# A hybrid mixer block on one core: a fifth pair of gate products by seven multiplications, sums moved into accumulating DMAs, and other steps at both ends

## The chip, the core and the metric

The kernel runs on one core of a Trainium2 chip. The core has a matrix engine (TensorE, PE in the profile; its weight loads are PEld), VectorE (DVE), ScalarE (ACT), GpSimd (POOL) and SyncE (SP). Each takes its own instructions in program order and waits on semaphores for the others. SP, ACT and POOL can issue DMAs, which run on 16 DMA engines. The metric is device microseconds of one execution; the time before is the median of three runs.

## What is computed

One decoder block for 256 tokens of width 2048, all in float32, cut to what matters here:

```python
def hybrid_mixer(h, w_in, ...):
    proj = jnp.einsum('bsd,de->bse', h, w_in)
    (q, k, v, g_out, gk_low, gate_b, gate_c, xc, merge_a, merge_b) = jnp.split(proj, SPLIT_IDX, axis=-1)
    ...
    y_a = (o * jax.nn.silu(g_out...))                                  # o: gated linear attention, normalised
    y_b = gate_b * causal_depthwise_conv(gate_c * xc, conv_w)          # y_t = sum_j w[j] u_{t-2+j}, j = 0..2
    merged = jax.nn.sigmoid(merge_a) * y_a + jax.nn.sigmoid(merge_b) * y_b
    return jnp.einsum('bse,ed->bsd', merged, w_out)

def swiglu(h, w_gate_up, w_down):
    gate, up = jnp.split(jnp.einsum('bsd,df->bsf', h, w_gate_up), [FFN_HIDDEN], axis=-1)
    return jnp.einsum('bsf,fd->bsd', jax.nn.silu(gate) * up, w_down)

h = x + hybrid_mixer(rmsnorm(x, mix_norm_w), ...)
h = h + swiglu(rmsnorm(h, ffn_norm_w), ...)
return rmsnorm(h, final_norm_w)
```

## The kernel before

**Weights as pieces.** All weights are read once or a little more, in pieces of 128 x 1024 floats (512 KB). A piece holds two row blocks of 128 for 512 columns (`n = 2`), or four for 256. Each piece is split for the matrix engine into a rounded high part `hi` (ScalarE, `high`, line 238) and a low part `lo = raw - hi` (VectorE, `low`, line 243), and each product is three matmuls, `mm3`, lines 347 to 349. `load_piece` runs up to five pieces ahead (`LOOK = 5`); there are five raw buffers, six for `hi`, five for `lo`.

**Entries and ticks.** `stream_list` lays down the order of all pieces. One piece used is one entry, and `used()` counts a tick after it. `later(d, f)` runs f's instructions d ticks on, `at(t, f)` at tick t, `one_at_a_time(d, f)` queues transposes that come d ticks on at the earliest and two ticks apart. These calls fix where an instruction stands in the program order of its engine. `pin` holds it there.

**Eights and sevens.** A group of 512 columns with 16 row blocks is done in one of two ways. As *eights* it has 8 entries of 12 matmuls (2 row blocks, 2 token blocks, 3 matmuls). As *sevens* two groups are done together by seven block products in place of eight: 28 entries of 6 matmuls. `seven_list` gives them in order: for each of four quarters q, 11, t1, t3, t2, t4, and then eight entries 21 and 22. The four t entries of a quarter are sums of weight blocks, formed on VectorE (lines 259 and 265) ahead of the split; the blocks for 21 and 22 are loaded a second time. So a pair of sevens has 24 loads and 16 sums, against 16 loads as eights. Its five accumulators `pa` to `pe` stand in PSUM banks b0 to b4, starting at bank 2n mod 5 for the n-th pair (`sevens`, line 402). Two are read at the end of the quarters, token block 1 being done after t4 of quarter 3 (`done(1, ...)`, line 429), token block 0 after the last entry (lines 435 and 436). `mixed` puts eights between the sevens: after each t entry, then after 21 and 22. Eights, down products and transposes use three other banks (`lent`); plain groups such as `wo0` take banks from a running count (`bank`, modulo 6, from wo0 on modulo 5).

**The gate stage.** For each of four blocks i of 512 columns there are six groups: gc and xc (their product is `us[i]`, the input of the convolution), gb, g, ma, mb. Four pairs (gc, xc) are sevens; everything else is eights. `gates_list` orders them by `GATES`: g0 alone, then each pair with 24, 24, 24 and 32 eights, and gb3 and mb3 alone at the end, 240 entries. When a pair is done, `conv(i)` copies `us[i]` one and two tokens down with six DMAs on POOL (lines 843 to 848) into `u1` and `u2`, and from 12 ticks on (`CONV_AT`) VectorE does three products with the taps and two adds (line 856). `merge(i)` multiplies by `sb[i]` (gb times the sigmoid of mb), adds `ya[i]` one tick later and queues two transposes of the result, which give `mh[i]`, `ml[i]` for the product with w_out. `wo0` follows as plain eights.

**The second half.** The other three wo groups, eight pairs of sevens (fg, fu) and the down products follow (`hidden_list`). A down product's two accumulators are added to the residual `h` by VectorE (line 1043). The last part of the down products runs alone (`down_list`), token block 0 ahead of 1 in its last group; `finish(t)` computes the last norm of a token block, scales and stores it in three parts.

**The start.** `hooks` puts the loads of x transposed (`start`) between the halves of the first weight piece (k0), and the small table `cols` behind the first of them on SP.

Of the kernel before, what the change touches and what calls it, by code (L numbers as in the profile page):

```python
# [8 lines left out]
F32 = mybir.dt.float32  # L9
# [3 lines left out]
ALU = mybir.AluOpType  # L13
# [30 lines left out]
def plan():  # L44
# [28 lines left out]
GATES = (  # L73
    (None, ("g0",)),
    (("gc0", "xc0"), ("ma0", "gb0", "mb0")),
    (("gc1", "xc1"), ("g1", "ma1", "gb1")),
    (("gc2", "xc2"), ("mb1", "g2", "ma2")),
    (("gc3", "xc3"), ("gb2", "mb2", "g3", "ma3")),
    (None, ("gb3", "mb3")),
)  # L80
# [26 lines left out]
def mixed(pair, eights, early=False):  # L107

    if pair is None:
        return eights  # L110
# [4 lines left out]
    while rest > 0:  # L115
        for some in (sums + ("11",) if early else sums, ("21", "22")):
# [68 lines left out]
def block_kernel(ctx, tc, x, xt, cols_in, gkw_in, gku_in, gnw, conv_w, finw, w_in, w_out, w_gu, w_dn, out):  # L185
# [82 lines left out]
    def load_piece():  # L268
# [4 lines left out]
        if i < len(stream):  # L273
            key, k0 = stream[i]
            if isinstance(k0, tuple):
                n, w = 2, 512
                raw = sum_of(key, *k0)
                step = n
            else:
# [3 lines left out]
                step = n // 2 if i == 0 else n  # L283
# [4 lines left out]
            else:  # L288
                if i == 0:
                    piece[1] = wlo.tile([P, n, w], F32R, tag="lo", name="lo")  # L290
                for a in range(0, n, step):
                    b = a + step
# [219 lines left out]
    def start(xs, a, b):  # L512
        nc.sync.dma_start(xs[:, 0:b - a, :], xt[:, a * T:b * T].rearrange("p (k t) -> p k t", t=T))
        if a == 0:
            nc.sync.dma_start(cols, cols_in)
# [17 lines left out]
    hooks[(0, 0)] = lambda: start(xs0, 0, 2)  # L533
# [299 lines left out]
    us, ya, sb, merge_at = {}, {}, {}, {}  # L833

    def conv(i):
        u = us[i]
# [4 lines left out]
        nc.gpsimd.memset(u1[0:1, 0, :], 0.0)  # L841
        nc.gpsimd.memset(u2[0:2, 0, :], 0.0)
        nc.gpsimd.dma_start(u1[1:113, :, :], u[0:112, :, :])
        nc.gpsimd.dma_start(u2[2:114, :, :], u[0:112, :, :])
        nc.gpsimd.dma_start(u1[113:128, :, :], u[112:127, :, :])
        nc.gpsimd.dma_start(u2[114:128, :, :], u[112:126, :, :])
        nc.gpsimd.dma_start(u1[0:1, 1, :], u[127:128, 0, :])
        nc.gpsimd.dma_start(u2[0:2, 1, :], u[126:128, 0, :])

        def taps_of(j):  # L850
            return taps[:, j:j + 1, :].to_broadcast([P, NT, 512])
# [326 lines left out]
```

## Time and profile before

| | us |
|---|---|
| median of 3 runs | 1507.53 (1506.82 to 1507.73) |
| the profiled execution, its own time | 1505.39 |
| its span, first to last instruction | 1503.7 |
| TensorE busy | 1488.9 |
| VectorE busy | 1277.6 |
| ScalarE busy | 862.9 |
| DMA traffic | 358.58 MB, 238 GB/s in the mean |

A busy time is the union of an engine's instructions. Matmuls overlap, so their lengths add up to more than TensorE's busy time. A row of the groups ("line engine op out<-in xcount | busy, mean ns | idle before, releaser") gives the sum and mean of one kind of instruction and what ended the idle time before it. A row of the windows gives the busy time of each engine in a stretch from the span's start. "us to landing" is from a DMA's issue to its last byte.

### The profile page before, as it was taken

Reading aid. Unit: us, or ns where it says so; the run is one execution under the profiler, and the core shown is the slowest. Engines: PE = TensorE matmul, PEld = TensorE weight load, DVE = VectorE, ACT = ScalarE, POOL = GpSimd, SP = SyncE. Lnnn points to the kernel's source line nnn. Section 1 sums busy time; section 2 is a strip of 40 time slices with the busy share of each in tenths; the row PEclk is TensorE's granted clock in tenths of the full one; section 3 lists DMA queues with packets and bytes.
Section 4 is the critical chain, followed back from the end, with each engine's and each line's share of the span. In section 5 each row is a group of like instructions: output and inputs, shape, how many; then the busy total and the mean of one; then the engine's idle time right before and its main releaser. Section 6 shows DMA issues by size and latency. Waiting matters only on the chain.

```text
span 1503.7 us, 19350 instructions
## 1 busy us (share of the span) xinstructions
PE 1488.9 (99%) x7057; PEld 1244.0 (83%) x7057; DVE 1277.6 (85%) x1280; ACT 862.9 (57%) x975; POOL 33.1 (2%) x60
## 2 busy tenths in 40 slices
PE   9999999999999999999999999999999999999997
PEld 8989988888887888888888888888888788888886
DVE  5885869979979879966689999999999999999975
ACT  6864546655655655654566756655565556565553
POOL 0010000000000000000000000000000000000000
PEclk9999999999999999999999999999999999999999
DMA  9755557877877877786676777777877777786782
GB/s 312 239 171 171 178 162 257 283 229 234 283 261 232 296 247 248 252 261 214 211 222 214 238 249 252 252 263 226 268 238 238 256 265 273 243 268 224 241 288 84
DMA packets 99984, 358.58 MB, mean 238 GB/s; under 512 B 11476, under 2 KB 11604, under 8 KB 99760
## 3 DMA queue, kind: packets, MB, share of 16 engines
q1 hardware_dynamic: 96656, 346.88, 70.0%
q0 software_dynamic: 2800, 8.89, 2.2%
q10 hardware_dynamic: 432, 1.57, 0.3%
q8 instruction: 55, 0.90, 0.2%
q14 instruction: 41, 0.34, 0.1%
HBM read 351.03 MB, written 2.10 MB: 235 GB/s over the span
## 4 chain that ended last, share of the span: by engine, by line
PE 95%; DVE 2%; issue 1%; ACT 1%; DMA 0%; SPq 0%; DVEq 0%; ACTq 0%
PE fg L347 8%; PE fg L349 8%; PE fg L348 8%; PE dn L347 5%; PE dn L349 5%; PE dn L348 5%; PE gc L347 3%; PE gc L348 3%; PE gc L349 3%; PE wo L347 2%; PE wo L349 2%; PE v L347 2%; PE gb L347 2%; PE wo L348 2%; PE v L348 2%; PE v L349 2%
## 5 line engine op out<-in xcount | busy, mean ns | idle before, releaser
L243 DVE TENSOR_TENSOR lo<-raw,hi 128x1024 fp32r<-128x1024 f32 (+1 forms) x505 | 611.6, 1219 | 114.3 <-ACT hi L238 32.3
L238 ACT CAST hi<-raw 128x1024 fp32r<-128x1024 f32 (+1 forms) x505 | 523.9, 1048 | 272.5 <-PE gb L349 25.9
L238 ACT CAST hi<-x 128x1024 fp32r<-128x1024 f32 x144 | 151.7, 1053 | 263.5 <-DVE x L265 201.0
L243 DVE TENSOR_TENSOR lo<-x,hi 128x1024 fp32r<-128x1024 f32 x144 | 176.1, 1223 | 37.8 <-ACT hi L238 26.3
L347 PE MATMUL dn<-lo,acth 128*128 128x512 f32 (+1 forms) x368 | 140.7, 382 | 1.7 <-DVE h L1043 0.9
L349 PE MATMUL dn<-hi,acth 128*128 128x512 f32 (+1 forms) x368 | 139.9, 380 | 0.0
L348 PE MATMUL dn<-hi,actl 128*128 128x512 f32 (+1 forms) x368 | 139.8, 380 | 0.0
L265 DVE TENSOR_TENSOR x<-x,raw 128x1024 f32<-128x1024 f32 x96 | 117.0, 1219 | 11.3 <-DMA raw<-in_w_in_dram 6.2
L347 PE MATMUL fg<-lo,hh 128*128 128x512 f32 x288 | 112.4, 390 | 0.0
L349 PE MATMUL fg<-hi,hh 128*128 128x512 f32 x288 | 112.2, 390 | 0.0
L348 PE MATMUL fg<-hi,hl 128*128 128x512 f32 x288 | 112.1, 389 | 0.0
L347 PE MATMUL fg<-lo,sh 128*128 128x512 f32 x256 | 101.0, 395 | 0.0
L348 PE MATMUL fg<-hi,sl 128*128 128x512 f32 x256 | 99.9, 390 | 0.0
L349 PE MATMUL fg<-hi,sh 128*128 128x512 f32 x256 | 99.8, 390 | 0.0
L347 PEld LDWEIGHTS dn<-lo,acth 128*128 128x128 f32 x368 | 69.2, 188 | 15.7 <-DVE h L1043 1.7
L349 PEld LDWEIGHTS dn<-hi,acth 128*128 128x128 f32 x368 | 69.2, 188 | 13.3
L348 PEld LDWEIGHTS dn<-hi,actl 128*128 128x128 f32 x368 | 69.2, 188 | 12.9
L347 PEld LDWEIGHTS fg<-lo,hh 128*128 128x128 f32 x288 | 54.1, 188 | 11.7 <-DVE lo L243 0.5
L349 PEld LDWEIGHTS fg<-hi,hh 128*128 128x128 f32 x288 | 54.1, 188 | 11.3
L348 PEld LDWEIGHTS fg<-hi,hl 128*128 128x128 f32 x288 | 54.1, 188 | 11.1
L259 DVE TENSOR_TENSOR raw<-y,x 128x1024 f32<-128x1024 f32 x48 | 58.5, 1219 | 4.4 <-DMA y<-in_w_gu_dram 2.5
L243 DVE TENSOR_TENSOR lo<-y,hi 128x1024 fp32r<-128x1024 f32 x48 | 58.5, 1218 | 4.3 <-ACT hi L238 2.2
(246 smaller groups left out, 3063.4 us busy)
## 6 DMA issues: line engine op xcount, KB each, us to landing
raw<-in_w_in_dram SPq DMA_DIRECT2D x255, 512.0 KB, 4.6
raw<-in_w_gu_dram SPq DMA_DIRECT2D x176, 512.0 KB, 4.4
raw<-in_w_dn_dram SPq DMA_DIRECT2D x88, 512.0 KB, 4.5
x<-in_w_gu_dram SPq DMA_DIRECT2D x32, 512.0 KB, 4.9
y<-in_w_gu_dram SPq DMA_DIRECT2D x32, 512.0 KB, 3.8
raw<-in_w_out_dram SPq DMA_DIRECT2D x32, 512.0 KB, 3.8
y<-in_w_in_dram SPq DMA_DIRECT2D x16, 512.0 KB, 4.6
x<-in_w_in_dram SPq DMA_DIRECT2D x16, 512.0 KB, 4.8
```

The lines of the kernel that those rows point to most:

```text
L238: nc.scalar.copy(hi[:, ks, :], raw[:, ks, :])
L243: nc.vector.tensor_tensor(out=lo[:, ks, :], in0=raw[:, ks, :], in1=hi[:, ks, :].bitcast(F32), op=ALU.subtract)
L259: nc.vector.tensor_tensor(out=raw, in0=y, in1=held["x"], op=ALU.add)
L265: nc.vector.tensor_tensor(out=x, in0=x, in1=other, op=ALU.add)
L347: nc.tensor.matmul(ps, lhsT=sh, rhs=ml, start=first, stop=False, skip_group_check=onto)
L348: nc.tensor.matmul(ps, lhsT=sl, rhs=mh, start=False, stop=False, skip_group_check=onto)
L349: nc.tensor.matmul(ps, lhsT=sh, rhs=mh, start=False, stop=last, skip_group_check=onto)
```

## The change

The gates: the list has five pairs in place of four. The fifth is (gb3, mb3), for which `gate_pair` had code already. The other 14 groups come in one order and are dealt out 21, 21, 21, 21 and 20 to a pair after g0; the list has 252 entries.

The convolution: `u1` is now u times tap 2; `u2` is u times tap 1, u itself is multiplied by tap 0, and both are added into `u1`, one and two tokens down, by three accumulating DMAs each on POOL. No memsets and no adds on VectorE are left. The products come 4 to 6 ticks after `conv`, and the multiplication by `sb`, now `convolved`, 20 ticks after the pair's end or when gb is there.

The merge: `ya` is added to `sb` by an accumulating DMA for i < 3, its transposes 8 ticks later in place of 3; for i = 3 by VectorE, with 2. `merge_later` holds a merge back until ma is done.

The down products of the first three parts are copied out by ScalarE and added to `h` by one accumulating DMA each.

The ends: the first piece is cut (1, 1, 2) in place of (2, 2), x likewise; `cols` is loaded from ScalarE's queue, ahead of x; a Sqrt of a spare cell stands three ticks into the last part; the last scaling is cut at 640, 1408 and 1792 in place of 512, 1024 and 1792.

```diff
-GATES = (
-    (None, ("g0",)),
-    (("gc0", "xc0"), ("ma0", "gb0", "mb0")),
...
-    (None, ("gb3", "mb3")),
-)
+GATES7 = ((("gc0", "xc0"), 21), (("gc1", "xc1"), 21), (("gc2", "xc2"), 21), (("gc3", "xc3"), 21), (("gb3", "mb3"), 20))
+GATES8 = ("g0", "ma0", "gb0", "mb0", "g1", "ma1", "gb1", "mb1", "g2", "ma2", "gb2", "mb2", "g3", "ma3")
...
 def gates_list():
-    return [e for pair, keys in GATES
-            for e in mixed(pair, [(key, k) for key in keys for k in range(0, KC, 2)], keys[0] == "gb2")]
+    plain = [(key, k) for key in GATES8 for k in range(0, KC, 2)]
+    out, plain = plain[:8], plain[8:]
+    for pair, n in GATES7:
+        out += mixed(pair, plain[:n])
+        plain = plain[n:]
+    return out + plain
...
-                step = n // 2 if i == 0 else n
+                cuts = (0, 1, 2, n) if i == 0 else (0, n)
...
     def start(xs, a, b):
+        if a == 0:
+            nc.scalar.dma_start(cols, cols_in)
         nc.sync.dma_start(xs[:, 0:b - a, :], xt[:, a * T:b * T].rearrange("p (k t) -> p k t", t=T))
-        if a == 0:
-            nc.sync.dma_start(cols, cols_in)
...
     def conv(i):
...
-        nc.gpsimd.memset(u1[0:1, 0, :], 0.0)
-        nc.gpsimd.memset(u2[0:2, 0, :], 0.0)
-        nc.gpsimd.dma_start(u1[1:113, :, :], u[0:112, :, :])
...
+        us[i] = u1
+        def tap(dst, j):
+            pin(nc.vector.tensor_tensor(out=dst, in0=u, in1=taps[:, j:j + 1, :].to_broadcast([P, NT, 512]), op=ALU.mult))
+        def add(src, s):
+            nc.gpsimd.dma_start(u1[s:112 + s, :, :], src[0:112, :, :], accum_op=ALU.add)
+            nc.gpsimd.dma_start(u1[112 + s:128, :, :], src[112:128 - s, :, :], accum_op=ALU.add)
+            nc.gpsimd.dma_start(u1[0:s, 1, :], src[128 - s:128, 0, :], accum_op=ALU.add)
+        later(TAPS_AT, lambda: tap(u1, 2))
+        later(TAPS_AT + 1, lambda: (tap(u2, 1), add(u2, 1)))
+        later(TAPS_AT + 2, lambda: (tap(u, 0), add(u, 2)))
+    def convolved(i, ts):
         v = sb[i][:, ts, :]
         pin(nc.vector.tensor_tensor(out=v, in0=v, in1=us[i][:, ts, :], op=ALU.mult))
-        later(1, lambda: pin(nc.vector.tensor_tensor(out=v, in0=v, in1=ya[i][:, ts, :], op=ALU.add)))
...
+    def merge(i, ts):
+        v = sb[i][:, ts, :]
+        if i < 3:
+            nc.gpsimd.dma_start(v, ya[i][:, ts, :], accum_op=ALU.add)
+        else:
+            pin(nc.vector.tensor_tensor(out=v, in0=v, in1=ya[i][:, ts, :], op=ALU.add))
...
-            one_at_a_time(3, lambda t=t: transpose_block(sb[i][:, t, :], t, mh[i], ml[i]))
+            one_at_a_time(2 if i == 3 else 8, lambda t=t: transpose_block(sb[i][:, t, :], t, mh[i], ml[i]))
...
+        nc.vector.tensor_scalar(out=h[:, t, 0:640], in0=h[:, t, 0:640], scalar1=r3, scalar2=None, op0=ALU.mult)
+        store(nc.sync, 0, 640)
+        nc.scalar.activation(h[:, t, 640:1408], h[:, t, 640:1408], AF.Copy, scale=r3)
+        store(nc.scalar, 640, 1408)
...
+        nc.vector.tensor_scalar(out=h[:, t, 1408:c0], in0=h[:, t, 1408:c0], scalar1=r3, scalar2=None, op0=ALU.mult)
+        store(nc.sync, 1408, D)
...
+        part = dpool.tile([P, NT, 512], F32, tag="sg8", name="part")
         for t in range(NT):
-            nc.vector.tensor_tensor(out=h[:, t, cs], in0=ps[t], in1=h[:, t, cs], op=ALU.add)
+            nc.scalar.copy(part[:, t, :], ps[t])
+        nc.gpsimd.dma_start(h[:, :, cs], part, accum_op=ALU.add)
...
+    later(3, lambda: pin(nc.scalar.activation(spare[:, 1:2], spare[:, 0:1], AF.Sqrt)))
...
-CONV_AT = 12
+TAPS_AT = 4
+CONV_AT = 14
```

More of the change, by code (lines that the diff above doesn't have):

```diff
@@ L115, in mixed @@
     while rest > 0:
-        for some in (sums + ("11",) if early else sums, ("21", "22")):
+        for some in (sums, ("21", "22")):
             for n, (_, e) in enumerate(sevens):
@@ L916, in done @@
                                                op0=ALU.mult, op1=ALU.mult)
-                later(3 if t else 1, lambda: merge(i, slice(t, t + 1)))
+                assert conv_at[i] <= count["tick"]
+                later(1, lambda: convolved(i, slice(t, t + 1)))
+                later(1, lambda: merge_later(1, i, slice(t, t + 1)))
         return second, done
```

58 lines of the change are left out of this document (26 added, 32 removed).

## The prediction

> **What bounds the kernel now.** I read the page first, then the windows of the gate stage, then the waits and the two ends.
>
> ```profile
> span 1503.7 us, 19350 instructions
> PE 1488.9 (99%) x7057; PEld 1244.0 (83%) x7057; DVE 1277.6 (85%) x1280; ACT 862.9 (57%) x975; POOL 33.1 (2%) x60
> PE 95%; DVE 2%; issue 1%; ACT 1%; DMA 0%; SPq 0%; DVEq 0%; ACTq 0%
> L347 PE MATMUL gb<-lo,xh 128*128 128x512 f32 x128 | 49.9, 390 | 0.0
> ...
> 230.00:330.00 100.00, 100.00 (x442) 1.00 0.79 257
> ```
>
> The chain that ended last is 95% TensorE. Nothing is idle there for long, so the time is a count of matmuls times their spacing. The last row is a window with TensorE alone (busy, count, clock, DMA share, GB/s): 442 matmuls in 100.00 us, 0.226 us from one to the next at clock 1.00. The 390 ns in the row above is the length of one, and successive ones overlap; the sum uses 0.226.
>
> The stage the change rewrites is the gates. Its windows are cut where a gate pair ends (columns: PE, PEld, DVE, ACT, POOL busy, clock, DMA share, GB/s):
>
> ```profile
> 228.00:332.50 104.50, 104.50 (x461) 86.26 (x461) 90.77 (x83) 63.09 (x66) 0.00 (x0) 1.00 0.77 253
> 332.50:438.00 105.50, 104.94 (x466) 86.25 (x466) 96.14 (x91) 60.76 (x64) 5.02 (x9) 1.00 0.78 257
> 438.00:543.50 105.50, 104.57 (x465) 86.08 (x464) 93.55 (x87) 60.17 (x63) 4.97 (x9) 1.00 0.77 258
> 543.50:668.50 125.00, 125.00 (x557) 103.30 (x556) 104.41 (x96) 70.34 (x72) 4.98 (x9) 1.00 0.80 257
> 668.50:712.00 43.50, 43.50 (x194) 35.97 (x193) 26.73 (x25) 20.10 (x22) 3.12 (x6) 1.00 0.75 223
> ```
>
> The rows are pairs 0 to 3 and then gb3, mb3 as eights. VectorE is at 0.87, 0.91, 0.89, 0.84 and 0.61. TensorE is idle 0.56 and 0.93 us in the two rows at 0.89 to 0.91, and not at all in the others: at about nine tenths VectorE begins to cost TensorE time.
>
> **The change part by part.**
>
> *The fifth pair.* As eights, gb3 and mb3 are 16 entries of 12 matmuls, 192; as sevens, 28 entries of 6, 168. 24 matmuls fewer x 0.226 = **-5.4 us**. The Trainium skill (Perfetto Trace Analysis, Identifying the Most-Contended Engine) calls matmul busy time a poor measure since matmuls are pipelined; by busy length the term would be 24 x 0.39 = 9.4 us, by spacing 5.4, and the trace agrees with the page.
>
> *VectorE in the gates.* Durations:
>
> ```profile
> L265 DVE TENSOR_TENSOR x<-x,raw 128x1024 f32<-128x1024 f32 x96 | 117.0, 1219 | 11.3 <-DMA raw<-in_w_in_dram 6.2 <-DMA raw<-in_w_gu_dram 4.6
> L243 DVE TENSOR_TENSOR lo<-x,hi 128x1024 fp32r<-128x1024 f32 x144 | 176.1, 1223 | 37.8 <-ACT hi L238 26.3 <-PE wo L347 4.1 <-PE gb L347 1.5
> L856 DVE TENSOR_TENSOR u<-u,u 128x1024 f32<-128x1024 f32 x8 | 9.7, 1216 | 0.0
> L862 DVE TENSOR_TENSOR sb<-sb,ya 128x1024 f32<-128x1024 f32 x4 | 4.9, 1218 | 0.0
> L435 DVE TENSOR_TENSOR u<-gc,v 128x512 f32<-128x512 f32 x4 | 2.7, 682 | 0.0
> ```
>
> Added: 16 sums and 12 more low parts at 1.22 = 34.2 us, and some 3.5 us to take the five accumulators out (seven 512-wide operations, the shape of the last row, for two). Removed: two adds for each of four convolutions, 8 x 1.22 = 9.7, and three merge adds, 3.7. Net +24 us, in a stage that gets 5.4 shorter. By pair: pairs 1 and 2 have 21 eights in place of 24, so they lose three low parts, two adds and one merge add, 7.3 us: 88.8 and 86.2 of VectorE in 105.5 - 36 x 0.226 = 97.4, that is 0.91 and 0.89 as before. What is new is that pairs 3 and 4 are now as full: pair 3 loses 11 eights' low parts (13.4) and two adds (2.4), 88.6 in 95; and the cover of the quiet last row goes. At 0.75 us lost per pair (mean of 0.56 and 0.93) and four such pairs, 3.0 in place of 1.5: **+1.5**. From below 0, from above +5, where the fifth, with 64 sums and low parts in 92 us, loses what all four do.
>
> *What waits at the fifth pair's end.* The accumulators of the fifth pair are banks b3, b4, b0, b1, b2 in the order pa to pe (it starts at 8 mod 5 = 3), and wo0 takes b4 and b0 (24 banks were handed out before it). So wo0's first matmul needs pb = b4, which is read only after the pair's last entry: one add of 0.68 us on VectorE, and the way there and back. Before, 16 eights stood between. The nearest rows are the wait for a bank of the down products, and one behind a low part:
>
> ```profile
> PE dn L347 <- DVE h L1043: 0.9, 2, 0.5
> PE g L347 <- DVE lo L243: 0.9, 1, 0.9
> ```
>
> I take **+0.9**, bounds 0.5 and 2.1 (a low part ahead of it). All of wo0 is queued behind it.
>
> *Accumulating DMAs.* Before, six plain copies go out together when a pair ends, and the taps' products follow 13 ticks later:
>
> ```profile
> 332.82 0.61 POOL L843 DMA_DIRECT2D u<-u  x1 [117.46 <-DVE u L908]
> 335.48 0.52 POOL L848 DMA_DIRECT2D u<-u  x1
> L856 DVE TENSOR_TENSOR u<-u,taps x12: 1214/1217/1221, 351.8 to 702.4; 128x1024 f32<-128x1024 f32 x12
> DMA to landing us min/median/max: 4.4/8.9/10.3
> taps<-in_conv_w_dram POOLq DMA_DIRECT2D x4, 768.0 KB, 11.1
> ```
>
> (The fourth row is for all DMAs that touch u.) The order now: from the pair's end, products at ticks 5, 6 and 7; three adding DMAs at 6, three more at 7, all on POOL; the sum multiplied by gb at tick 20. The second three add to the bytes of the first, so POOL holds them until those have landed. The Trainium skill (DMA: Bandwidth & Descriptors, Rules for kernel authors) says the same: an accumulate reads its destination and writes it later with nothing holding the bytes between, so the next must wait for the first one's semaphore. No run here shows it yet; without it the chain would be about 13 us, with it about twice that.
>
> The chain goes by the copies' rows: issue 1.6 (three at 0.53), landing 8.9, issue 1.6, landing 8.9: 21 us. Ticks 6 to 20 after pair 0 hold 8 sevens (1.36 each, 6 x 0.226) and 6 eights (2.71): 27 us. Cost nothing, VectorE's other work covering it, as long as a landing stays below some 12 us. An accumulate reads its destination too, so a landing between once and twice the copy's is my bound. The taps load was issued long before by POOL, which has nothing else queued; it stays hidden.
>
> The tight place is pair 3. Its convolution's adds go out at ticks 209 and 210, and the DMA that merges ya2 into sb2, at 213, is queued on POOL behind the second add, which waits for the first. The transposes of sb2 are due at 221. From 209 to 221 there are 7 sevens and 5 eights, 23.1 us; POOL's chain is 21 + 0.6 = 21.6 with plain landings (merge and second add fly together). TensorE runs in order, so a late merge stops all of it. At 1.5 times the landing: 30.5, 7 us late; at twice, 16. The first add has only half the bytes of the six copies in flight, so I expect less than 8.9 for it. **+1.0**, bounds 0 and +16. Merges 0 and 1 have POOL to themselves and 16 to 18 us; the fourth stays on VectorE, its transposes two ticks later and three entries (8 us) ahead of wo0's use.
>
> DMA engines: 23 accumulated half-megabytes, of which 12 replace copies or come spread over the down products, and 8 more loads, beside a share of 0.77 to 0.80: at nothing, the five raw buffers cover it; without that cover each late load would show as ScalarE's wait.
>
> *Down products.* 24 adds of 0.68 leave VectorE, 24 copies come to ScalarE (57% busy) and twelve DMAs to POOL. Both free a bank at the same point; the part's buffer is shared with the next product, 6 eights and some 11 sevens (31 us) later. **-0.3**, a third of the 0.9 above; bounds -0.9 and +0.5.
>
> *The end.*
>
> ```profile
> 1491.91 0.43 DVE L1108 TENSOR_TENSOR h<-dn,h 128x256 f32<-128x256 f32 x1 [1.12 <-PE dn L349]
> 1492.96 1.28 ACT L986 ACT_TABLE_LOAD   x1
> 1494.47 0.28 PE L349 MATMUL dn<-hi,acth 128*128 128x256 f32 x1
> 1495.58 0.61 DVE L995 TENSOR_SCALAR h<-h,r 128x768 f32<-128x768 f32 x1
> 1496.11 0.42 DVE L1108 TENSOR_TENSOR h<-dn,h 128x256 f32<-128x256 f32 x1
> 1499.07 0.33 SPq L996 DMA_DIRECT2D out_dram<-h  x1
> out_dram<-h SPq DMA_DIRECT2D x2, 512.0 KB, 3.5
> out_dram<-h SPq DMA_DIRECT2D x2, 256.0 KB, 2.4
> ```
>
> The last half's add starts at 1496.11 though TensorE is done at 1494.75: VectorE is behind with the first half, late by the table load of 1.28. With the Sqrt table loaded early (ScalarE is idle between its casts there) it starts at about 1494.8: -1.3. The last product shrinks from 768 to 384 columns and the first grows to 640: -0.1. The last store goes from 512 to 320 KB, about 2.7 (between 2.4 and 3.5), but ScalarE's 768 columns now end no earlier and its store is larger: -0.4. **-1.8**, bounds -1.3 and -2.2.
>
> *The start.*
>
> ```profile
> 0.82 0.38 SPq L513
> 1.26 0.42 SPq L515
> 3.62 5.89 DMA raw<-in_w_in_dram
> 9.53 1.06 ACT hi L238
> 11.89 0.38 PE q L348
> ```
>
> TensorE streams from 11.89 on, when q0's first piece is split, and that piece is issued at 3.62, seventh on SP. Cutting the first piece in three adds two issues to SP and the move of cols to ScalarE's queue takes one off, so it goes out one issue (0.47) later. Earlier first matmuls gain nothing, since q0's landing ends the stage. **+0.2**, bounds -0.3 and +0.6.
>
> **Sum.** -5.4 + 0.9 + 1.5 + 1.0 - 0.3 - 1.8 + 0.2 = **-3.9 us**. It is made against the profiled execution's 1505.39 (span 1503.7 and 1.7 around it), which gives 1501.5. The shown median, 1507.53, lies 2.1 above that execution; the same difference gives **1503.6**.
>
> **Rivals.**
>
> *A, slower: POOL's chain is late.* If an accumulate lands in 1.5 to 2 times the copy's 8.9, pair 3's merge stops TensorE for 7 to 16 us, and at twice the multiplications at tick 20 of pairs 0 and 1 come some 12 us late each, half of it covered by the five pieces ahead. That is +7 to +28 on 1502.6: 1510 to 1531, about 1515 at 1.7 times. It decides from 1.2 times on. For it: the waits are serial on one queue at DMA share 0.8. Against: half the bytes in flight.
>
> *B, no change: VectorE doesn't hold five full pairs.* At 0.91 a burst (pair end, taps, gated) finds no quiet stretch after it; at 1.7 us more per pair than I took, 2.5 us in each, the gain is 0 to 1: 1507. For it: +24 us of VectorE. Against: pair 0, at 0.87, loses nothing.
>
> *C, more gained.* All small losses at their lower bounds: -5.4 + 0.5 - 1.8 - 0.3 - 0.2 = -7.2: 1500.3. For it: the adds taken off VectorE are those in its densest bursts.
>
> **Chances.** Forecast 0.50 (its own range 1501 to 1506), A 0.24, B 0.14, C 0.12. A measurement of this kernel can tell about 0.2%, 3.0 us, from no change. Faster by more: 0.40 of the forecast, 0.12 of C, 0.02 of A: 0.54. Within: 0.10, B's 0.08, 0.02 of A: 0.20. Slower: A's 0.20 and B's 0.06: 0.26. Range 1500 to 1513: the lower part of A is in it, its upper part and a little of C are out.
>
> **What would show it.** Right: 7033 matmuls; 24 adds to h gone from VectorE; TensorE idle at the start of wo0 for about a microsecond behind line 435's add; the table load gone from before the last Sqrt. A shows as TensorE's transposes of sb waiting for a DMA, or VectorE's multiply of sb by u1 doing so, near the fifth pair. B shows as matmuls waiting for lo throughout the five pairs. The forecast is wrong if transposes wait over 3 us in all, or if TensorE's idle time in the gates is over 6.

## The result and the profile after

The changed kernel takes 1522.76 us (median of 4 runs, 1521.43 to 1524.78); the kernel before took 1507.22 beside it. By these medians that is 15.5 us slower, where 4 us faster was forecast, and it lies above the range. The measured ratio is 1.0108, with a 95% interval of 1.0095 to 1.0121; that of the two medians, 1.0103, lies inside it. The profiled execution took 1524.78 and its span is 1523.0. All medians and ratios below are over fast runs, which leaves out one execution of 4029.4 us among run 13's four.

The first question is in which stage the 19.3 us between the spans lie. The rows of the tiles show it: each gives the first and last start of a group of matmuls (columns: line, engine, operation, count, durations in ns, first to last start in us, shape). First the kernel before, the accumulators v, gc, wo, fg and dn; the last row is of the page's DMA queues (packets, MB, share of the engines):

```profile
L347 PE MATMUL v<-lo,xh x128: 389/389/476, 34.8 to 203.6; 128*128 128x512 f32 x128
L347 PE MATMUL gc<-lo,sh x128: 389/389/497, 229.4 to 665.4; 128*128 128x512 f32 x128
L347 PE MATMUL wo<-lo,mh x128: 389/389/499, 712.3 to 821.1; 128*128 128x512 f32 x128
L347 PE MATMUL fg<-lo,hh x288: 388/389/494, 752.5 to 1435.7; 128*128 128x512 f32 x144
L349 PE MATMUL dn<-hi,acth x368: 279/389/398, 988.7 to 1494.5; 128*128 128x512 f32 x168, 128*128 128x256 f32 x16
q0 software_dynamic: 2800, 8.89, 2.2%
```

The changed kernel, the same rows:

```profile
L342 PE MATMUL v<-lo,xh x128: 389/389/476, 35.2 to 204.0; 128*128 128x512 f32 x128
L342 PE MATMUL gc<-lo,sh x128: 389/389/481, 229.9 to 630.4; 128*128 128x512 f32 x128
L342 PE MATMUL wo<-lo,mh x128: 388/389/504, 732.9 to 841.1; 128*128 128x512 f32 x128
L342 PE MATMUL fg<-lo,hh x288: 388/389/499, 772.4 to 1456.6; 128*128 128x512 f32 x144
L344 PE MATMUL dn<-hi,acth x368: 279/389/397, 1008.6 to 1515.5; 128*128 128x512 f32 x168, 128*128 128x256 f32 x16
q0 software_dynamic: 6496, 16.76, 5.7%
```

| stage, by these starts | before | after | difference |
|---|---|---|---|
| first instruction to v | 34.8 | 35.2 | +0.4 |
| v to gc | 194.6 | 194.7 | +0.1 |
| gates, gc to wo | 482.9 | 503.0 | +20.1 |
| wo0, wo to fg | 40.2 | 39.5 | -0.7 |
| fg to the last dn | 742.0 | 743.1 | +1.1 |
| last dn to the span's end | 9.2 | 7.5 | -1.7 |

The whole loss is in the gates, which were to get shorter by 5.4 us less what waits there. Everything outside them adds to -0.8.

The windows of that stage, cut where the pairs would end without any loss (the first ends there, the later ones come 5 to 16 us later, and the stage goes on to 732.9; columns as in the prediction: PE, PEld, DVE, ACT, POOL busy, clock, DMA share, GB/s):

```profile
229.00:325.00 96.00, 96.00 (x425) 79.51 (x424) 84.80 (x77) 59.01 (x61) 0.00 (x0) 1.00 0.78 255
325.00:422.00 97.00, 93.24 (x407) 76.50 (x407) 84.72 (x80) 54.32 (x58) 6.87 (x8) 0.98 0.81 257
422.00:519.00 97.00, 93.01 (x404) 76.45 (x403) 83.04 (x77) 51.50 (x54) 6.75 (x8) 0.96 0.80 254
519.00:617.00 98.00, 92.78 (x401) 76.08 (x401) 81.56 (x76) 53.03 (x55) 5.84 (x7) 0.98 0.78 244
617.00:712.00 95.00, 90.01 (x390) 74.09 (x390) 83.17 (x77) 53.02 (x55) 5.92 (x7) 0.96 0.79 250
```

The first row has no convolution in it yet, five pairs' density all the same, and TensorE is never idle. In the four rows behind it TensorE is idle for 3.8 to 5.2 us each, and VectorE isn't busier there but less busy. What waits is in the view of waits (us in total, times, longest); the first row is of the kernel before, for comparison with the third:

```profile
DVE raw L259 <- DMA y<-in_w_in_dram: 1.8, 2, 1.1
...
POOL u L846 <- DMA u<-u: 20.8, 4, 7.2
DVE raw L256 <- DMA y<-in_w_in_dram: 13.6, 6, 4.4
PE gc L342 <- DVE lo L240: 13.0, 3, 5.2
PE trb L567 <- DMA sb<-ya: 5.0, 1, 5.0
```

TensorE has three stops of matmuls behind a low part and one of transposes behind the merge's accumulating DMA. VectorE's wait for y grew from 1.8 to 13.6 us; ScalarE's for `raw`, which has five buffers, did not (11.0 before, 10.0 after, in the same stretch). One stop of each kind in the chain of waits (start, length, what):

```profile
345.60 1.23 DVE x L262
346.85 9.69 DMA y<-in_w_in_dram
...
357.77 1.23 DVE lo L240
359.04 0.50 PE gc L342
...
360.74 0.43 PE g L342
...
656.26 12.59 DMA sb<-ya
668.89 1.12 PE trb L567 x4
```

`y` holds the first piece of a pair's block, in one buffer (line 228: two for x, one for y). Its load goes out when VectorE has read the old one for the last time, at 346.83, and lands 9.69 us later; then come the low part and the matmul. The DMA view from 338 to 360 us tells what it meets (packets, MB, share; then the median time to landing):

```profile
q1 hardware_dynamic: 1064, 3.83, 49.4%
q0 software_dynamic: 592, 1.83, 40.8%
...
raw<-in_w_in_dram SPq DMA_DIRECT2D x5, 512.0 KB, 10.3
taps<-in_conv_w_dram POOLq DMA_DIRECT2D x1, 768.0 KB, 12.4
y<-in_w_in_dram SPq DMA_DIRECT2D x1, 512.0 KB, 9.7
```

POOL's queue q0, with the adds and the next taps, takes 40.8% of the engines for 1.83 MB, the weights 49.4% for 3.83 MB: a megabyte on q0 holds them 1.7 times as long. Loads that land in 4.5 us on the page take 10. Here q0's taps load went out between the two sets of adds (338.99; the sets at 336.73 and 345.30). After such a stop a run of matmuls starts 0.43 us apart in place of 0.226 (here eight of them, six matmuls after the stop), and the window that holds them shows a lower clock:

```profile
350.00:355.00 5.00, 5.00 (x24) 4.03 (x22) 1.60 (x2) 2.00 (x2) 0.00 (x0) 1.00 1.00 284
355.00:360.00 5.00, 1.24 (x6) 0.83 (x5) 3.37 (x3) 3.04 (x3) 0.00 (x0) 1.00 0.68 251
360.00:365.00 5.00, 5.00 (x17) 3.95 (x16) 4.95 (x6) 1.36 (x2) 0.00 (x0) 0.66 0.60 165
```

From the starts of matmuls in the trace: the four stops (4.15, 4.38, 5.61, 5.38 us) are 18.6 us beyond the normal spacing, the matmuls at 0.43 behind them another 7.3, and all other gaps 1.8. The sum, 27.7, is counted from the spacing of a run without the convolution, which comes below.

### The profile page after: what moved, and what is told of

Read it like the earlier page. It is cut to its first block, busy times and chain, and to the rows that moved or that the text cites. A ratio compares the mean times of both kernels' runs of the same rounds, so it can differ in the third digit from the quotient of the medians.

```text
span 1523.0 us, 19424 instructions
## 1 busy us (share of the span) xinstructions
PE 1491.6 (98%) x7033; PEld 1246.0 (82%) x7033; DVE 1288.1 (85%) x1281; ACT 888.6 (58%) x1012; POOL 58.3 (4%) x67
## 4 chain that ended last, share of the span: by engine, by line
PE 90%; DMA 5%; DVE 2%; issue 1%; ACT 1%; SPq 0%; POOL 0%; DVEq 0%; ACTq 0%; POOLq 0%
PE fg L342 8%; PE fg L344 8%; PE fg L343 8%; PE dn L342 5%; PE dn L344 5%; PE dn L343 5%; PE gc L342 3%; PE gc L344 3%; PE gc L343 3%; DMA y<-in_w_in_dram 2%; PE wo L342 2%; PE v L343 2%; PE v L342 2%; PE wo L344 2%; PE wo L343 2%; PE v L344 2%
## 5 line engine op out<-in xcount | busy, mean ns | idle before, releaser
L235 ACT CAST hi<-x 128x1024 fp32r<-128x1024 f32 x156 | 164.3, 1053 | 289.8 <-DVE x L262 224.7
L240 DVE TENSOR_TENSOR lo<-x,hi 128x1024 fp32r<-128x1024 f32 x156 | 190.8, 1223 | 36.3 <-ACT hi L235 25.2
L262 DVE TENSOR_TENSOR x<-x,raw 128x1024 f32<-128x1024 f32 x104 | 126.8, 1219 | 15.2 <-DMA raw<-in_w_in_dram 12.4
L256 DVE TENSOR_TENSOR raw<-y,x 128x1024 f32<-128x1024 f32 x52 | 63.4, 1219 | 17.6 <-DMA y<-in_w_in_dram 13.6
L240 DVE TENSOR_TENSOR lo<-y,hi 128x1024 fp32r<-128x1024 f32 x52 | 63.3, 1218 | 6.0 <-ACT hi L235 2.1
L262 DVE TENSOR_TENSOR x<-x,y 128x1024 f32<-128x1024 f32 x52 | 63.5, 1221 | 1.0
L235 ACT CAST hi<-y 128x1024 fp32r<-128x1024 f32 x52 | 54.6, 1049 | 16.6 <-DMA y<-in_w_in_dram 8.3
```

The lines of the kernel that those rows point to most:

```text
L235: nc.scalar.copy(hi[:, ks, :], raw[:, ks, :])
L240: nc.vector.tensor_tensor(out=lo[:, ks, :], in0=raw[:, ks, :], in1=hi[:, ks, :].bitcast(F32), op=ALU.subtract)
L256: nc.vector.tensor_tensor(out=raw, in0=y, in1=held["x"], op=ALU.add)
L262: nc.vector.tensor_tensor(out=x, in0=x, in1=other, op=ALU.add)
```

## The experiments

The letters in the expectations: T, the accumulating transfers fill the DMA engines and make the loads beside them late; S, the serial order on POOL's queue costs, whatever the transfers do; C, the one buffer of y is the missing cover; V, VectorE can't hold five full pairs (B among the prediction's rivals); P, the pairs' own order and density cost. In the table, "gates" is from the first start of gc to the first of wo in the profiled execution, and the last column is how much longer that is than without any convolution, 475.3, where TensorE is busy all the time and no two starts are over 0.32 us apart. Each figure of the gates is of one execution, and the executions of a run differ by 1 to 8 us in their whole time, so differences of 2 or 3 us between two runs' gates say little.

| run | median, us | ratio to before, interval | gates | over 475.3 |
|---|---|---|---|---|
| before | 1507.22 | | 482.9 | four pairs |
| changed | 1522.76 | 1.0108 (1.0095-1.0121) | 503.0 | 27.7 |
| 1 sums as plain copies | 1513.74 | 1.0050 (1.0034-1.0066) | 491.1 | 15.8 |
| 2 taps apart | 1511.21 | 1.0035 (1.0022-1.0047) | 491.8 | 16.5 |
| 3 merge on VectorE | 1519.27 | 1.0086 (1.0068-1.0105) | 500.0 | 24.7 |
| 4 no accumulating DMA in the gates | 1508.69 | 1.0021 (1.0011-1.0031) | 488.1 | 12.8 |
| 5 two y buffers | 1515.85 | 1.0064 (1.0050-1.0078) | 492.9 | 17.6 |
| 6 taps apart, transposes later | 1510.02 | 1.0024 (1.0010-1.0037) | 487.0 | 11.7 |
| 7 before, new end | 1505.09 | 0.9993 (0.9984-1.0002) | | |
| 8 before, down products' sums by DMA | 1506.46 | 1.0002 (0.9993-1.0011) | | |
| 9 no convolution | 1497.19 | 0.9941 (0.9926-0.9956) | 475.3 | 0 |
| 10 four pairs, all accumulating DMAs | 1516.31 | 1.0065 (1.0046-1.0084) | 493.1 | four pairs |
| 11 products only | 1499.82 | 0.9955 (0.9941-0.9970) | 478.9 | 3.6 |
| 12 transfers only | 1500.52 | 0.9962 (0.9947-0.9977) | 476.7 | 1.4 |
| 13 products spread | 1513.49 | 1.0056 (1.0035-1.0078) | 494.2 | 18.9 |
| 14 VectorE's five operations spread | 1516.92 | 1.0067 (1.0044-1.0091) | 493.4 | 18.1 |
| 15 products on POOL | 1531.68 | 1.0171 (1.0157-1.0185) | 508.3 | 33.0 |
| 16 the same, old start | 1528.53 | 1.0151 (1.0138-1.0165) | 507.3 | 32.0 |
| 17 plain pieces behind the pair | 1500.88 | 0.9966 (0.9954-0.9979) | 479.3 | 4.0 |
| 18 the same, no accumulating DMA | 1520.02 | 1.0093 (1.0078-1.0108) | 498.6 | 23.3 |

**Runs 1 to 4: one suspect at a time.**

Run 1, in `add`, so that the sums of the convolution are left out:

```diff
-src[0:112, :, :], accum_op=ALU.add)
+src[0:112, :, :])
```

> The changed kernel with the convolution's six DMAs as plain copies into the same bytes, with the same waits and the same order (the shifted sums are left out, so u1 is only copied over). Theory T: an accumulated packet holds its DMA engine about twice as long as a copied one, and that is what makes the weight loads beside it land 10 us late; then the three waits for y at the convolutions of blocks 0, 1 and 2 (4.2, 4.4 and 5.6 us, with about 2 us at half clock behind each) shrink to under 1 us each, and the time is 1503 to 1510. Rival S: it is the serial order, the second three held back until the first have landed, that puts them beside the loads; then the waits stay and the time is 1517 to 1523.

Run 2:

```diff
-        nc.gpsimd.dma_start(taps, conv_w[...])
+        if i < 3:
+            later(30, lambda: load_taps(i + 1))
```

> The changed kernel with the load of the next block's taps (768 KB, which POOL issued between the two sets of adds) held back by 30 ticks. Theory T, with the DMA engines full for some 15 us: 0.77 of 2.8 MB leave the burst, each wait for y shrinks by 2 to 5 us, time 1509 to 1517. Rival S, or if the adds alone are enough to fill the engines: within 2 us of the changed kernel, 1520 to 1524.

Run 3, in `merge`:

```diff
-        if i < 3:
-            nc.gpsimd.dma_start(v, ya[i][:, ts, :], accum_op=ALU.add)
-        else:
-            pin(nc.vector.tensor_tensor(...))
+        pin(nc.vector.tensor_tensor(out=v, in0=v, in1=ya[i][:, ts, :], op=ALU.add))
...
-            one_at_a_time(2 if i == 3 else 8, ...)
+            one_at_a_time(2, ...)
```

> The changed kernel with the three merge sums on VectorE again and their transposes two ticks later. Both theories: the one stop of TensorE for sb<-ya (5.2 us idle and 2 us at half clock) goes, 1514 to 1517. If instead time is lost on VectorE, which gets 3.7 us more, 1520 or over.

Run 4 has run 3's merge and the convolution of the kernel before: copies at the pair's end, five operations of VectorE 12 to 16 ticks later.

> Five pairs with no accumulating DMA in the gates: convolution and merges as before on VectorE, the down products still accumulated, the new ends. Theory T and S: all four stops go; what is left is the matmuls (5 us less) and the end (1.7 us less): 1500 to 1505. Rival B, that VectorE doesn't hold five pairs without the relief: matmuls wait for low parts throughout the five pairs, 1507 to 1520.

Run 1 lies between T's and S's figures: the same transfers without the read of the destination save 11.9 us of the gates, but all three y stops stay, shorter (2.06, 2.84 and 4.56 us). Run 2 saves 11.2 by the place of one plain load: the y stops fall to 1.34 us and less. What counted was that the load no longer stands between the two sets of adds. The first is 22 us behind the second set, but the other two go out right behind it, at 448.92 and 546.63. Run 3 takes the transposes' stop away, and only 3.0 of the 7.3 us that it and the slow matmuls behind it had cost come back; the three y stops are as they were (5.01, 4.38 and 5.30 us). Run 4 is the first that speaks for V: no long stop is left and still 12.8 us are lost, in gaps of 0.5 to 2.7 us, most of them behind VectorE's results, and 3.4 of them in matmuls at 0.43.

**Runs 5 and 6.** A second y buffer costs space that one of the two `ya` buffers gave; run 6 is run 2 with 16 ticks in place of 8 between merge and transposes, which puts the merge ahead of its use.

```diff
-            held["y"] = fetch(one, 4 * q, held["pool"], "y")
+            held["y"] = fetch(one, 4 * q, *((ew, "yb") if one[:2] in ("gc", "gb") and q % 2 else (held["pool"], "y")))
-                    ya[i] = ew.tile([P, NT, 512], F32, tag=f"ya{i % 2}", name="ya")
+                    ya[i] = ew.tile([P, NT, 512], F32, tag="ya", name="ya")
```

> The kernel with the merges on VectorE (e3), with a second buffer for y, used in turn (its 4 KB come from ya, which has one buffer in place of two). Theory C: what turns slow loads into stops is that y has one buffer, is asked for only when its last reader is done, and holds up SP's later loads; then the waits for y (4.9, 4.3 and 5.2 us) fall under 1.5 us each and the time is 1503 to 1511. Rival D: the DMA engines are full for 15 us, and any load would be late; then the waits turn up at raw loads and the time is within 4 us of e3, 1516 to 1522.

> The kernel with the taps' load apart (e2), with the transposes 16 ticks behind an accumulated merge in place of 8. Theory: the wait of the transposes for sb<-ya (3.0 us in e2, about 2 us at half clock behind it) goes, 1506 to 1509. If VectorE's backlog stands behind it, the time stays at 1510 to 1512.

The y stops of run 5 fall from 4.4 to 5.3 us (run 3) to 0.7 to 1.8: with cover the late load costs little. But matmuls now wait for `ya` and `sb` of VectorE (3.4 and 2.3 us), so the run can't say what the buffer is worth. Run 6 has no stop over 2.3 us and no matmul at 0.43, and is left with 11.7 us. Its matmuls and transposes wait 5.3 us for VectorE's `ml` and `ya`, and 3.4 for low parts.

**Runs 7 and 8, the parts outside the gates.** The end's lines alone, and the twelve accumulating DMAs of the down products alone, put into the kernel before.

> The kernel before with the new end alone (Sqrt's table early, the last scaling cut at 640 and 1408). Every theory: 1.5 to 2.0 us less than before, since nothing else touches the last 10 us.

> The kernel before with the down products copied out by ScalarE and accumulated into h. As predicted (their DMAs are spread, 31 us apart): within 1 us of before. If an accumulating DMA delays the loads beside it here too, 2 to 6 us slower.

The end gives 1.3 us in the medians, within the interval's reach of nothing; the down products give nothing.

**Runs 9 and 10: which of the two?** Run 9 is the changed kernel with its transposes 16 ticks behind the merge and no convolution: `sb` is multiplied by u itself, with no taps, products or sums. Run 10 has the four pairs and the order of before with all the accumulating DMAs.

```diff
     def conv(i):
-        u1 = ew.tile(...)
...
-        later(TAPS_AT + 2, lambda: (tap(u, 0), add(u, 2)))
+        pass
```

> The changed kernel with the transposes 16 ticks behind an accumulated merge (as in e6) and the convolution left out: no taps, no products, no shifted DMAs, sb is multiplied by u itself. VectorE loses 3.7 us per block and the DMA burst is gone. Theory V: what e4 and e6 still lose in the gates (12 to 13 us in place of 2.8) is VectorE, which with five full pairs has no slack for bursts; then that loss falls under 5 us and the time is 1500 to 1504. Rival P: it is the order of the entries or the banks of five pairs; then it stays at 10 us or more, 1507 to 1511.

> The changed kernel with the four pairs and the order of before, and all accumulating DMAs (the multiplication of the last block 16 ticks after its pair in place of 20). Theory T: the burst of adds and taps meets the loads of the pairs behind it here too, so TensorE stops for y at the convolutions of blocks 0, 1 and 2, 1514 to 1522. If the stops need the fifth pair's fuller VectorE, three quarters of them go: 1504 to 1509.

The tile rows of run 9:

```profile
L342 PE MATMUL gc<-lo,sh x128: 389/389/481, 229.6 to 610.3; 128*128 128x512 f32 x128
L342 PE MATMUL wo<-lo,mh x128: 389/389/501, 704.9 to 813.1; 128*128 128x512 f32 x128
```

Five pairs, with all their sums and low parts, lose nothing: 475.3 us, where 482.9 - 5.4 = 477.5 would be before's own loss kept. The window of its fullest stretch has VectorE at 0.91 and TensorE never idle:

```profile
325.00:422.00 97.00, 97.00 (x433) 80.35 (x432) 87.80 (x82) 58.75 (x62) 1.02 (x1) 1.00 0.77 250
```

So V in its first form falls, and the convolution is the whole loss. Run 10 shows the other side: the accumulating DMAs cost four pairs 10.2 us too (493.1 - 482.9). But its y stops are two, of 1.6 us, where five pairs had three of 4.2 to 5.6; its longest, 2.98 and 2.94 us, are transposes that wait for VectorE's `ml`. So the time came out in T's range without the stops that T named: the long ones needed the fifth pair's order or its work as well.

**Runs 11 and 12: the convolution cut in two.** Run 11 adds to run 9 the three products per block (u by u: no taps, no shifts), run 12 the taps loads and the six accumulating DMAs (onto zeros; no products). Run 12 doesn't have its transfers where the changed kernel has them: with no product to read the taps, all four loads go out before the first pair's end, and the adds go out as soon as u is there (POOL, start, length):

```profile
246.13 0.76 POOL L837 DMA_DIRECT2D taps<-in_conv_w_dram  x1 [8.93 <-DMA taps<-in_conv_w_dram]
329.18 0.95 POOL L842 DMA_DIRECT2D u<-u  x1 [82.29 <-DVE u L923]
```

In the changed kernel the first add follows line 430's addition at the pair's end (324.7) by 12 us, in run 12 (326.1) by 3. So run 12 prices the two sets of adds alone, at another place, and not the burst with the taps in it.

```diff
-        later(TAPS_AT, lambda: tap(u1, 2))
-        later(TAPS_AT + 1, lambda: (tap(u2, 1), add(u2, 1)))
-        later(TAPS_AT + 2, lambda: (tap(u, 0), add(u, 2)))
+        later(TAPS_AT, lambda: tap(u1))
+        later(TAPS_AT + 1, lambda: tap(u2))
+        later(TAPS_AT + 2, lambda: tap(u))
```

> As the run without a convolution (1497.2 us against 1506.4 for the kernel before), but the three products of each block are issued by VectorE again, at their places and of their size, with no taps, no shifted sums and no transfer of the convolution: its shifts and taps are left out, the products multiply the gate by itself. Theory V (VectorE's bursts of three products of 128x1024 on top of five full pairs let the weight splits and the releases of the banks come late): 1503 to 1508, stops of 0.6 to 2.7 us in the gates behind sb, ml and ya of VectorE, excess of TensorE in the gates 6 to 12 us. Theory T (the convolution's loss is its transfers): 1496 to 1500, excess below 3 us.

> The counterpart: the taps load and the six accumulating transfers of each block at the places of the changed kernel (onto zeros that POOL writes), and no product: the taps are left out of the sum. Theory T: the three stops behind the late weight loads come back, with 2 us each at half clock behind them, 1506 to 1512, excess in the gates 9 to 15 us. Theory V: the transfers alone cost little while VectorE has slack to catch up, 1497 to 1502. The two runs' losses over 1497.2 should add to about those of the changed kernel with its merge late.

Run 11, products only:

```profile
L342 PE MATMUL gc<-lo,sh x128: 388/389/481, 230.4 to 611.9; 128*128 128x512 f32 x128
L342 PE MATMUL wo<-lo,mh x128: 388/389/499, 709.3 to 817.5; 128*128 128x512 f32 x128
```

Run 12, transfers only:

```profile
L342 PE MATMUL gc<-lo,sh x128: 389/389/481, 230.2 to 612.3; 128*128 128x512 f32 x128
L342 PE MATMUL wo<-lo,mh x128: 388/389/501, 706.9 to 815.1; 128*128 128x512 f32 x128
```

Theory V's number didn't come: 3.6 us with the products. The 1.4 of run 12 can't decide on T, as its taps are out of the way. The two make 5.0 together (6.0 by the medians), where run 6, which has both, with two of its taps loads right behind the adds, loses 11.7 (12.8 by the medians), and the changed kernel 27.7. It looks as if the two didn't just add, but the places of the transfers differ too, and no run has the changed kernel's transfers without its products. Where they could meet is seen in the changed kernel's waits of SP's queue in the gates:

```profile
SPq L290 <- DVE lo L240: 154.4, 75, 7.3
SPq L229 <- DVE lo L240: 133.5, 71, 6.7
```

SP holds each next load (line 290 the pieces of the eights, 229 those of the pairs) until VectorE has made the low part of an earlier piece and so given its buffer back. VectorE's products could so make the loads go out later, and POOL's transfers make them land later, while the lead of the buffers covers either alone. That this loop is the cause is argued, not shown: run 9, which loses nothing, has waits as long in these two rows (161.1 and 111.5 us up to 712, against 140.9 and 130.3 in the changed kernel).

**Runs 13 and 14: spread.** If bursts were the matter, the same operations apart should help: products 8 ticks apart in run 6's kernel, and run 4's five operations 5 ticks apart.

```diff
-        later(TAPS_AT + 1, ...)
-        later(TAPS_AT + 2, ...)
+        later(TAPS_AT + 8, ...)
+        later(TAPS_AT + 16, ...)
```

> The changed kernel with its whole computation: taps 40 places later, the transposes 16 places behind the merge, and now the three products of a block 8 places apart in place of one each place, the multiplication by them 14 places later than it was. With the products together the same kernel took 1510.0 (excess 11.9 in the gates). If VectorE's burst is what is left (theory V), 1500 to 1505, excess 2 to 6; if it is VectorE's sum of work over the pair, or the transfers, no better than 1508.

> The five pairs with the convolution as it was before the change (copies and five operations of VectorE; 1508.7 with these five together, excess 12.9), but its five operations 5 places apart, the multiplication 12 places later. Burst (theory V): 1500 to 1505. Sum of VectorE's work in a full pair: 1507 to 1511, as two more operations of each block stay on VectorE than in the spread accumulating kernel.

Both got slower, by 7.2 and 5.3 us in the gates, so spreading the burst doesn't take the loss away. Their longest stops, 5.01 and 4.05 us, are matmuls that wait for VectorE's `ya` and `sb`. Why spreading is worse stays open.

**Runs 15 and 16: the products on another engine.** Run 6's kernel with `nc.gpsimd.tensor_tensor` in `tap` and the multiplication 6 ticks later; run 16 also has the start of the kernel before.

> The whole computation, taps 40... the taps load 30 places later, the transposes 16 places behind the merge (1510.0 us so far), and the three products of a block on POOL in place of VectorE, the multiplication by their sum 6 places later. Theory X (neither VectorE's products nor the transfers cost much alone, 2.6 and 3.3 us over 1497.2, but together they take the lead of the loads): with the products off VectorE the gates come near those with the transfers alone, excess 2 to 6 us, 1499 to 1504. If POOL's products slow VectorE down, or if the multiplication and the merge of VectorE's and the transfers are enough for the loss, 1506 to 1512.

> The same with the start of the kernel before (the first piece cut in two halves, the per-column values on SP's queue): first v matmul 0.3 to 0.6 us earlier than in the other run, everything after it the same, so 0.3 to 0.6 us less; the medians may not show it.

The worst of all, and the timeline says why. VectorE beside POOL's products (start, length):

```profile
327.78 1.21 DVE L240 TENSOR_TENSOR lo<-x,hi 128x1024 fp32r<-128x1024 f32 x1
328.91 3.42 DVE L240 TENSOR_TENSOR lo<-raw,hi 128x1024 fp32r<-128x1024 f32 x1
332.26 3.41 DVE L262 TENSOR_TENSOR x<-x,raw 128x1024 f32<-128x1024 f32 x1
...
336.87 4.10 DVE L240 TENSOR_TENSOR lo<-x,hi 128x1024 fp32r<-128x1024 f32 x1
```

POOL in the same stretch:

```profile
327.95 6.63 POOL L852 TENSOR_TENSOR u<-u,taps 128x1024 f32<-128x1024 f32 x2 [112.73 <-DVE u L936]
...
336.63 3.24 POOL L852 TENSOR_TENSOR u<-u,taps 128x1024 f32<-128x1024 f32 x1
```

For each of POOL's three products one operation of VectorE takes 3.4 to 4.1 us in place of 1.21: a product moved to POOL takes more of VectorE's time (2.2 to 2.9 us) than it did on VectorE (1.22). The Trainium skill (SBUF — State Buffer, Terms) has the port pair of the two engines as held for a whole instruction, with the loser blocked; the trace agrees. So the run doesn't decide on the meeting of products and loads, it makes VectorE later. Run 16's first v matmul starts 0.9 us before run 15's. All runs together say the same of the start: with the new one it lies at 35.65 us in the median of 14 kernels (34.9 to 37.4), with the old one at 34.65 in six (34.6 to 35.3).

**Runs 17 and 18: room behind the pair.** Five of each pair's 21 plain pieces (eights) stand alone behind the pair, where the next convolution begins: a plain piece asks VectorE for one low part in 12 matmuls, a piece of the pair for a low part and up to one sum in 6. Run 17 is run 6's kernel with this and the old start, run 18 run 4's with this, the old start and transposes 16 ticks behind.

```diff
     for pair, n in GATES7:
-        out += mixed(pair, plain[:n])
+        alone = 5 if plain[n:] else 0
+        out += mixed(pair, plain[:n - alone]) + plain[n - alone:n]
         plain = plain[n:]
```

> The whole computation with five pairs and accumulating transfers, taps 30 places later, transposes 16 behind the merge, the start of the kernel before; and five of each pair's 21 plain pieces now stand alone behind the pair, where the block's three products are due, so that VectorE and the loads can catch up there. Theory X (products and transfers meet a VectorE that frees the loads' buffers with no lead to give): excess in the gates falls from 11.9 to 2 to 6 us, 1499 to 1504. If the denser rest of the pair (16 plain pieces beside the same seven products) costs as much as the catching up gives: 1508 to 1513.

> The same five pairs with five plain pieces behind each, but no accumulating transfer in the gates: convolution by plain copies and five operations of VectorE, merges on VectorE, transposes 16 places behind them, the start of the kernel before. With the pieces mixed in and the transposes 2 places behind it took 1508.7 (excess 12.9). Theory X: 1500 to 1505, excess 3 to 8. If VectorE's work in the pair is the bound whatever its places: 1507 to 1511.

Run 17 beats both kernels: 1500.88 us, 0.9966 (0.9954 to 0.9979) of the kernel before, with the whole computation. Its tile rows:

```profile
L343 PE MATMUL gc<-lo,sh x128: 389/389/481, 229.3 to 600.4; 128*128 128x512 f32 x128
L343 PE MATMUL wo<-lo,mh x128: 388/389/499, 708.6 to 816.8; 128*128 128x512 f32 x128
```

The gates take 479.3 us, 7.7 less than run 6 for the pieces' places (the start lies outside), with the products in a burst still, and with DMA shares of 0.82 to 0.86 in the last four windows (0.79 to 0.85 in run 6). VectorE's sum of work over the stage is that of run 6, so it wasn't this sum that cost. Run 18, with the five operations 12 to 16 ticks behind the pair and so past the free stretch, went the other way. Around one late load in it (issued at 600.15, landed 5.64 us later) the plain pieces themselves run slowly, VectorE's timeline:

```profile
610.92 1.22 DVE L241 TENSOR_TENSOR lo<-raw,hi 128x1024 fp32r<-128x1024 f32 x1 [1.46 <-PE gb L343]
614.85 1.22 DVE L241 TENSOR_TENSOR lo<-raw,hi 128x1024 fp32r<-128x1024 f32 x1 [2.71 <-PE mb L343]
618.78 1.22 DVE L241 TENSOR_TENSOR lo<-raw,hi 128x1024 fp32r<-128x1024 f32 x1 [2.71 <-PE mb L343]
```

A low part waits 2.71 us for the matmuls that read an earlier one, they wait 1.22 for it: a piece takes 3.93 us in place of 2.71, and no lead comes back as long as that lasts. My reading is that plain pieces give room only when they are met with a lead. Runs 17 and 18 differ in the transfers, in the merge, and in the number and places of VectorE's operations; which of these decides was not tried.

## Why the prediction failed

- *The step that failed*: "DMA engines: [...] at nothing, the five raw buffers cover it", and with it a price for each transfer's lateness but none for the traffic it is to others. The five buffers cover `raw`, not `y`, which has one; its load lay beside the 40.8% that q0 took, and three stops of 4 to 6 us with slow matmuls behind them followed. The taps load, priced as hidden since POOL has nothing queued before it, now lay between the two sets of adds: its place alone is worth 11.2 us (run 2). The prediction named ScalarE's wait as the sign of lost cover; that stayed (10.0 us, 11.0 before), and it came as VectorE's wait for y, 13.6 us. Moving the taps load and the transposes takes back 16.0 of the 27.7 us (run 6). The other 11.7 come from the convolution too (run 9), but how products and transfers make them stays open.
- *Rival A* had the direction, and its 1510 to 1531 holds the time, but by luck: it had the wrong place for most of it. Its mechanism, a late merge that stops the transposes, is there: the sum landed after 12.59 us, 1.4 times the copy's 8.9, and TensorE stopped for 5.38. With the slow matmuls behind it that is 7.3 us where +1.0 was taken; the bounds, 0 to 16, held it. Taking the merge away gave 3.0 (run 3).
- *Serial adds on POOL*: right, `POOL u L846 <- DMA u<-u` is 20.8 us in four waits. The adds of 448 KB landed in 8.2 us in the median (10.5 in the set beside the taps), the copies of that size before in 7.4, and the sum had taken 8.9, the median of all six copies. No wait of VectorE for the sum is in the view: the convolution's own chain cost nothing, as forecast. The kernel keeps the Trainium skill's rule cited there (DMA: Bandwidth & Descriptors, Rules for kernel authors), and this wait is what that takes; no run shows what is lost without it.
- *VectorE +1.5 in the gates*: near, but by luck: with the products and no transfers the gates take 478.9, 1.4 over 482.9 - 5.4. The reading behind it, that VectorE at nine tenths begins to cost TensorE time, doesn't hold: run 9 has it at 0.91 with no time lost. And with transfers beside it the same work is part of a loss of 11.7 to 27.7 us, so that pricing it by itself may have been the wrong form. Rival B is refuted by run 9 as far as five full pairs alone go.
- *The fifth pair, -5.4*: borne out; 7033 matmuls, and run 9's gates are 7.6 us shorter than before's with no idle time left.
- *wo0's bank, +0.9*: didn't occur. wo0's first matmul starts at 732.86, 0.24 us behind the pair's last and ahead of the add at 733.42 that it was to wait for. Its first six matmuls start before that add ends (734.10); I take them to be those of the other token block, whose bank is free, but the profile doesn't name the block. Wo to fg is 0.7 us shorter.
- *Down products, -0.3*: that stretch is 1.1 longer in the profiled execution, the run alone is the same within 0.1%: too small to tell.
- *The end, -1.8*: -1.7 by the rows; run 7 alone gives 1.3 in the medians. *The start, +0.2*: +0.4 in the profiled execution, but 1.0 in the medians over all kernels, above its bound of +0.6.

The test set in the prediction, transposes waiting over 3 us or TensorE idle over 6 in the gates, was met by both (5.0 us in the transposes, 18.0 in the gates).

## What to carry to other kernels

Before a transfer is priced at nothing, look for the smallest buffer among the loads that it will meet, not the largest: here the single-buffered one stopped the engine. Where loads are released by the engine that also gets the new work, don't trust a sum of separate prices; here the products alone cost 3.6 us, and with the transfers beside them the loss was 11.7 or more. And where both were wanted, in the form of run 17, making room at the place where they fall was worth more than spreading them or moving the products to another engine.

## What the runs showed of the hardware

- An accumulated half megabyte took 8.4 us from issue to landing in the median of the merge's three and 12.59 in one; in the trace's records its 4096-byte packets hold an engine for 327 ns, plain ones for 159 to 171. Over the run q0 moved 1.9 times as many bytes as before, for 2.6 times the share (5.7% against 2.2%).
- After every stop of TensorE of 3.6 us or more between two starts, in the gates of the runs, 6 to 12 matmuls started 0.43 us apart, 1.2 to 2.4 us more in all. After 2.3 to 3.4 us this sometimes came (after 2.27 us in run 4, 2.33 in run 14) and sometimes didn't (after 3.21 us in run 15); after less it never came. The Trainium skill (TensorE: Matmul & The Clock Gate, Part 1: The HAM clock gate) gives a free-running window of about 3.4 us without work for the fall to half rate and as much for the return. The return agrees (0.43 us apart from 360.74 on, 0.23 again at 364.11: 3.4 us). For the fall the measurements differ: in run 4 TensorE was idle for 1.78 us in that stop, and half rate followed.
- A two-input operation of POOL on 128x1024 took 2.40 to 3.37 us beside VectorE's work (3.30 in the median of run 15's twelve), and in the stretch shown each held up one operation of VectorE, which took 3.4 to 4.1 us in place of 1.21.
